# A convolution and gate taken through PSUM by halves, and a product left in its bank until its sums

## The chip, the cores and the metric

The kernel runs on one core of one Trainium2 chip. The metric is the device time of one execution in microseconds (us); what is quoted for a kernel is the median of its runs. The engines have short names in the profile: PE is TensorE's matrix products (PEld its weight loads), DVE is VectorE, ACT is ScalarE, POOL is GpSimd, SP is SyncE, which here only issues DMAs. PSUM has eight banks of 128 partitions by 512 float32 numbers; products land there, VectorE and ScalarE read and write it, POOL does not use it in this kernel.

## The reference, cut to what matters

One layer of a decoder trunk on 2048 tokens of 1024 features. The change touches its feed-forward part alone:

```python
h = h + conv_ffn(rms_norm(h, ln2_g), w_up, conv_w, conv_b, w_down)
return rms_norm(h, lnf_g)

def conv_ffn(h, w_up, conv_w, conv_b, w_down):
    up = h @ w_up                              # 1024 -> 2 * 2816
    up = causal_depthwise_conv(up, conv_w)     # three taps along the tokens
    up = up + conv_b
    gate, val = up[..., :2816], up[..., 2816:]
    return (silu(gate) * val) @ w_down         # 2816 -> 1024
```

Ahead of it stand the input projection, attention over a window, and a state space model; they are not changed.

## The kernel before, in words

The program is one long list of instructions for each engine. A scheduler that knows the dependences puts them in order ahead of time by modelled durations; on the chip each engine runs its own list strictly in order and waits at semaphores. Buffers come from pools: a tile of a name gets the next free buffer of that name, and its first writer waits for the last user of the buffer's previous tile.

The kernel runs in passes. Passes A to D make the input projection, state space and attention, with h, the tokens after attention, kept in device memory. Pass E is the feed-forward up to the product of gate and value, pass F the product down and the last norm.

In E and F every matrix product is cut in two along each dimension and computed with seven products of blocks instead of eight (Winograd's form of Strassen's method). The seven are M1 to M7, in the order M1, M5, M6, M7, M2, M3, M4 (`n` = 0 to 6 in `pair`). One operand is fixed for a pass (r0 to r6, built by `fixed` from blocks loaded into the staging buffers sg0 and sg1, both `sg` in the profile), the other comes by steps (`moving`, sums in the tile `sums`). Each operand is float32 and is split into a high and a low half (`split`: a cast on ScalarE, a subtraction, here on POOL for the steps' operands); a product of blocks is therefore 12 matrix instructions of 512 columns where four blocks are summed over (9 where three are). The split halves of the steps' operands go around five buffer sets: sq, ath, atl, xt, ln.

Pass E goes over two halves of 1024 tokens, and in each over 22 steps of 128 gate and 128 value features, taken in pairs: 11 pairs a half. Pass F goes over three groups of features (blocks of 4, 4 and 3), each over 8 steps of 256 tokens, again in pairs. So there are 22 pairs in E and 12 in F, with the fixed operands replaced four times on the way. `pass_of` runs a pass; while its last pair's products run, the next pass's fixed operands are built one after the other behind the last product that uses the old one (`nxt` in `pair`).

`pair` puts each product into a PSUM bank (eight banks taken in rotation, L1057) and takes it out again: M1 and M5 are copied by ScalarE (L1075), the others are added by VectorE to a running sum in SBUF (L1078). After M7, C12 gets M5 by an addition on POOL (L1080) and C22 by one on VectorE (L1081), both between SBUF tiles. The places c are halves of the tiles u: `yl` (gate) and `sm_` (value) of 1024 tokens and two tokens before.

`up_end` runs the convolution for a step: for gate and value a first tap with bias on ScalarE into a tile `xh` (L1148), two more taps on VectorE (L1149, L1150, listed as L118), Silu of the gate on ScalarE (L1151), the product of both on VectorE (L1152, listed as L115), and one store to `act_d`. Lines 115, 118 and 133 are helpers (`tt_`, `stt_`, `split`), so many instructions of the profile carry these lines, and are told apart by their tiles. In F, `more` adds the tokens h (tile `xh`) to the sums, two quarters on VectorE and two on POOL.

Of the kernel before, what the change touches and what calls it, by code (L numbers as in the profile page):

```python
# [9 lines left out]
F32 = mybir.dt.float32  # L10
# [6 lines left out]
P = 128  # L17
L = 2048
D = 1024
# [22 lines left out]
def constants():  # L42
    """Tables that depend on shapes alone: identity, band masks, shifts, rotary angles."""
# [25 lines left out]
def trunk(ctx, tc, a, out):  # L69
# [50 lines left out]
    def rstd_of(ss, n):  # L120
        """1/sqrt(ss/n + eps): a power refined by one Newton step."""
# [9 lines left out]
    def split(hi, lo, x, eng=None):  # L131
        """x as the sum of two numbers that the tensor engine takes whole."""
        S.copy(out=hi, in_=x)  # L133
        tt_(lo, x, f(hi), ALU.subtract, eng)

    # ================ pass A: first norm, input projection; the state space's matrices ================
# [49 lines left out]
    def norm_in(g):  # L186
        """Normed tokens, turned, as exact halves."""
# [42 lines left out]
    def proj_qkv(b, hi, lo):  # L230
# [14 lines left out]
        # rotary on the first 16 of each head's features  # L245
# [8 lines left out]
        # queries and keys as exact halves: a head's halves side by side, the keys' each twice  # L254
# [7 lines left out]
        # values and their differences to the block before  # L262
# [14 lines left out]
    def pass_a(g):  # L277
        """A pair of blocks: its state space's input, and queries, keys and values of the pair before."""
        hnT[g] = norm_in(g)
        if 0 < g < NB // 2 - 1:  # L280
            both_qkv(g - 1)
        proj_u(g, *hnT[g])
# [10 lines left out]
    # heads of a group: the even ones, then the odd ones  # L293
# [76 lines left out]
    # sine and cosine: to the nearest multiple of pi/2, then by polynomials  # L370
# [26 lines left out]
    # by quadrant: swapped where odd, then signs  # L397
# [16 lines left out]
    # powers 0..8 of the discrete eigenvalues  # L414
# [22 lines left out]
    # input matrices, (lam_bar - 1) / lam times b  # L437
# [19 lines left out]
    # by half of the partitions (real parts, imaginary parts)  # L457
# [12 lines left out]
    # phase of a chunk, doubled seven times  # L470
# [6 lines left out]
    # two groups to a table: the first's phases on the lower partitions, the second's on the upper  # L477
# [26 lines left out]
    def tables(j):  # L504
        """Cosines and sines, cosines and negated sines of a chunk's phase by its number, for two groups."""
# [17 lines left out]
    def matrices(j):  # L523
        """A chunk's matrices, for GB groups: input to state, state to output; for twice as many,
        input to output."""
# [54 lines left out]
    # ================ pass B: the state space; attention and its part of the output ================  # L580
# [26 lines left out]
    def ssm(j):  # L607
        """The state space for GB groups."""
# [66 lines left out]
    def padded(t, x, kv, r):  # L675
        """A head's values on one half of the partitions to be, zeros on the other."""
# [3 lines left out]
    def attention(b):  # L680
# [5 lines left out]
        for kv in range(NKV):  # L686
            # key slots: this block's where it is no later than the query, else the previous one's
# [37 lines left out]
            else:  # L725
                # all weights on the previous block's values, this block's weights on the differences
# [18 lines left out]
    def attention_in(b):  # L745
        (q, k), idr = qkvs.pop(b), idrs[0]
        # turned: a head's halves of queries over each other, against its group's keys' halves, twice each
# [36 lines left out]
    # values between zeros: a head's product lands on the lower or the upper half of the partitions  # L784
# [11 lines left out]
    def out_half(th, tl, wh, wl, done, nms=("pi", "pi")):  # L796
        """Rows of one half of the output projection for a block of tokens."""
# [16 lines left out]
    def sumsq(t):  # L814
        """Squares of a block's features, for their sums by token."""
# [28 lines left out]
    def load_gate():  # L844
        """Weights of the state space's gate and of its half of the output projection."""
# [89 lines left out]
    # ================ pass D: the state space's gate, its part of the output, second norm ================  # L935
# [345 lines left out]
```

## Time and profile before

| | us |
|---|---|
| three runs | 2229.15 to 2231.34, median 2230.11 |
| span of the profiled execution, first to last instruction | 2223.6 |
| the profiled execution's own time | not given apart from its span |
| PE busy | 2034.0 (91%) |
| DVE busy | 1810.5 (81%) |
| POOL busy | 1473.9 (66%) |
| ACT busy | 1002.3 (45%) |
| mean granted clock of TensorE | 0.961 of full speed |

Busy time is the sum of the durations of an engine's instructions, including any time in which an instruction was held up while it ran. The page's slices of the span show PE at 9 tenths in most of the second half, with dips near 1220 to 1300, 1680 to 1770 and 1890 to 1940 us. Pass E begins at about 781 us, between the last parts of D, its second half at about 1253, and F at about 1717.

### The profile page before, as it was taken

The page shows a single profiled execution, that of the slowest core. Times are in us where ns is not written, and L with a number is a line of the kernel's source. Part 1 is how long each engine was busy: PE and PEld are TensorE (multiplying, and loading weights), DVE is VectorE, ACT ScalarE, POOL GpSimd, SP SyncE. Part 2 cuts the span into 40 slices and gives each one's busy share as a digit, 9 for nine tenths or more (in the row PEclk, how much of TensorE's full clock was granted, in tenths as well). Part 3 has the DMA queues.
Part 4 walks back from the last instruction along what each step waited for, and adds up shares of the span by engine and source line. Part 5 has one row for each costly group of instructions (what it writes and reads, how often), then busy time and mean ns, then how long its engine had stood idle before and what let it go on. Part 6 is the DMA issues. An engine that isn't in the chain of part 4 may idle for free.

```text
span 2223.6 us, 29721 instructions
## 1 busy us (share of the span) xinstructions
PE 2034.0 (91%) x10057; PEld 1695.7 (76%) x10057; DVE 1810.5 (81%) x2491; ACT 1002.3 (45%) x2007; POOL 1473.9 (66%) x1247
## 2 busy tenths in 40 slices
PE   7899977999899889999999789999997899899896
PEld 6789967888788778887777568878776687688664
DVE  6987368999876768878788987878889968767898
ACT  5575346555556544434434343444434423233333
POOL 2556325766631556676776976776778879888985
PEclk9999988999999999999999899999999899899998
DMA  7476386777556752232332323231323455464543
GB/s 213 155 259 251 125 276 221 223 230 217 160 173 202 216 169 71 82 90 67 92 108 69 121 76 96 67 103 59 122 86 122 149 184 171 170 218 148 183 156 139
DMA packets 304621, 335.49 MB, mean 151 GB/s; under 512 B 92070, under 2 KB 237910, under 8 KB 302934
## 3 DMA queue, kind: packets, MB, share of 16 engines
q1 hardware_dynamic: 304470, 333.60, 46.7%
q8 instruction: 80, 1.31, 0.2%
q14 instruction: 71, 0.58, 0.1%
HBM read 214.14 MB, written 119.41 MB: 150 GB/s over the span
## 4 chain that ended last, share of the span: by engine, by line
PE 29%; DVE 16%; POOL 9%; issue 6%; DMA 4%; ACT 2%; DVEq 0%; ACTq 0%; SPq 0%; POOLq 0%
PE pz L1071 7%; PE ps L1071 7%; DVE xh L118 6%; PE po L1071 4%; PE pi L1071 4%; PE px L1071 3%; PE pp L1071 3%; DVE sums L115 3%; DMA yh<-in_w_up_dram 2%; POOL yl L115 1%; POOL atl L115 1%; POOL ath L115 1%; ACT xh L1148 1%; POOL sq L115 1%; POOL ln L115 1%
## 5 line engine op out<-in xcount | busy, mean ns | idle before, releaser
L1148 ACT ACTIVATE xh<-yl,cb,cw 128x1024 f32<-128x1024 f32 x44 | 54.8, 1245 | 244.6 <-DVE yl L115 144.7
L118 DVE SCALAR_TENSOR_TENSOR xh<-yl,cw,xh 128x1024 f32<-128x1024 f32 x88 | 145.5, 1653 | 13.3 <-ACT xh L1148 12.2
L115 POOL TENSOR_TENSOR rs<-rs,mhalf 128x1 f32<-128x1 f32 x80 | 51.8, 654 | 157.3 <-DVE rs L112 151.1
L115 POOL TENSOR_TENSOR atl<-sums,atl 128x512 fp32r<-128x512 f32 (+1 forms) x40 | 68.2, 1705 | 30.1 <-ACT atl L133 30.0
L115 POOL TENSOR_TENSOR ln<-sums,ln 128x512 fp32r<-128x512 f32 (+1 forms) x43 | 70.0, 1627 | 24.4 <-ACT ln L133 20.0
L115 POOL TENSOR_TENSOR sq<-sums,sq 128x512 fp32r<-128x512 f32 (+1 forms) x42 | 73.2, 1743 | 19.4 <-ACT sq L133 18.7
L115 POOL TENSOR_TENSOR xt<-sums,xt 128x512 fp32r<-128x512 f32 (+1 forms) x39 | 58.8, 1508 | 33.1 <-ACT xt L133 33.1
L1151 ACT ACTIVATE xh<-xh 128x1024 f32<-128x1024 f32 x44 | 46.7, 1062 | 72.2 <-DVE xh L118 72.2
L115 DVE TENSOR_TENSOR sums<-yt 128x512 f32<-128x512 f32 (+1 forms) x48 | 64.8, 1352 | 16.5 <-POOL xt L115 7.1
L115 DVE TENSOR_TENSOR xh<-xh 128x1024 f32<-128x1024 f32 x44 | 76.2, 1732 | 1.8
L218 PE MATMUL pz<-hnT_lo,wu_h 128*128 128x256 f32 x256 | 73.8, 291 | 2.6 <-DVE hnT_lo L115 2.6
L218 PE MATMUL pz<-hnT_hi,wu_h 128*128 128x256 f32 x256 | 72.1, 291 | 2.1 <-ACT hnT_hi L133 2.0
L218 PE MATMUL pz<-hnT_hi,wu_l 128*128 128x256 f32 x256 | 72.7, 287 | 0.0
L115 POOL TENSOR_TENSOR sq<-sq 128x256 f32<-128x256 f32 (+1 forms) x64 | 42.5, 678 | 41.6 <-ACT sq L817 41.1
L115 POOL TENSOR_TENSOR vv<-vv 128x255 f32<-128x255 f32 x32 | 26.3, 822 | 64.6 <-DVE vv L115 59.5
L115 POOL TENSOR_TENSOR ath<-sums,ath 128x512 fp32r<-128x512 f32 (+1 forms) x40 | 64.6, 1615 | 5.0 <-ACT ath L133 5.0
L115 DVE TENSOR_TENSOR sums<-yt,yh 128x512 f32<-128x512 f32 x44 | 48.1, 1093 | 23.0 <-DMA yh<-in_w_up_dram 21.9
L115 DVE TENSOR_TENSOR sg<-sg,sg 128x2048 f32<-128x2048 f32 (+1 forms) x20 | 54.9, 2743 | 13.3 <-DMA sg<-in_w_down_dram 8.6
L709 ACT ACTIVATE s<-s,m 128x128 f32<-128x128 f32 x120 | 46.9, 392 | 40.8 <-DVE m L118 40.8
L804 PE MATMUL pi<-w_oh,ath 128*128 128x512 f32 x128 | 55.1, 430 | 7.4 <-DVE rs L112 5.3
L115 POOL TENSOR_TENSOR mh<-th,cc 128x512 fp32r<-128x512 f32 x30 | 42.0, 1400 | 24.9 <-ACT th L133 24.8
L115 POOL TENSOR_TENSOR atl<-yh,atl 128x512 fp32r<-128x512 f32 (+1 forms) x29 | 47.6, 1642 | 15.3 <-ACT atl L133 9.7
(1963 smaller groups left out, 8294.5 us busy)
## 6 DMA issues: line engine op xcount, KB each, us to landing
xh<-h_d SPq DMA_DIRECT2D x48, 512.0 KB, 4.3
yt<-in_w_up_dram SPq DMA_DIRECT2D x44, 512.0 KB, 4.6
yh<-in_w_up_dram SPq DMA_DIRECT2D x44, 512.0 KB, 3.7
act_d<-xh SPq DMA_DIRECT2D x44, 512.0 KB, 3.1
h_d<-yl SPq DMA_DIRECT2D x32, 512.0 KB, 3.7
qk_d<-qx SPq DMA_DIRECT2D x16, 768.0 KB, 3.2
sg<-h_d SPq DMA_DIRECT2D x12, 1024.0 KB, 6.8
sg<-in_w_down_dram SPq DMA_DIRECT2D x12, 1024.0 KB, 5.8
```

Of the source, the lines that this page charges most:

```text
L115: (eng or V).tensor_tensor(out=o, in0=x, in1=y, op=op)
L118: V.scalar_tensor_tensor(out=o, in0=x, scalar=s, in1=y, op0=o0, op1=o1)
L218: E.matmul(out=pu, lhsT=l["u"][:, k, cs], rhs=r[:, k, :], start=n == 0, stop=n == 3 * KT - 1)
L709: S.activation(out=s[:, h], in_=s[:, h], func=AF.Exp, bias=m[:, h:h + 1], accum_out=den[:, h:h + 1])
L804: E.matmul(out=po, lhsT=l[:, k, :], rhs=r[k][:, cs], start=n == 0, stop=n == 11)
L1071: E.matmul(out=b, lhsT=l[:, k], rhs=r[:, k], start=m == 0, stop=m == 3 * kh - 1)
L1148: S.activation(out=v, in_=u[s_][:, 2:], func=AF.Identity, scale=w2, bias=cb[:, fc_:fc_ + 1])
L1151: S.activation(out=ds[0], in_=ds[0], func=AF.Silu)
```

## The change

In `pair`, a product's bank is chosen by its number: M5 (`n == 1`) and M3 (`n == 5`) take `pi` and `po` in turn, all others `ps` and `pz` in turn, of which there are two buffers each. `pp` and `px`, one buffer each, are left to the convolution. M5 is no longer copied out; its bank is kept until M7 is there, and both sums with M5 are then made by VectorE from the bank. In the last step of F both sums were on VectorE before, too.

In `up_end` the convolution runs by halves of 512 tokens. The first tap goes to the bank `pp` (gate) or `px` (value), the other two taps run on VectorE from bank to bank, Silu reads `pp` and writes SBUF, the product reads `px` and writes SBUF.

```diff
-    banks, turn = ("pz", "ps", "pi", "po", "pz", "ps", "pp", "px"), [0]
-
-    def pair(ops, res, cs, nxt=None, more=None, eng=None):
+    turn = [0, 0]
+
+    def mm_bank(n):
+
+        k = int(n == 1)
+        turn[k] += 1
+        return bank((("ps", "pz"), ("pi", "po"))[k or n == 5][turn[k] % 2], [P, HF])
+
+    def pair(ops, res, cs, nxt=None, more=None):
+
+        m5 = {}
...
-                b = bank(banks[turn[0] % 8], [P, HF])
-                turn[0] += 1
+                b = mm_bank(n)
...
-                if n < 2:
-                    S.copy(out=c[3 * n], in_=b)
+                if n == 0:
+                    S.copy(out=c[0], in_=b)
+                elif n == 1:
+                    m5[s_] = b
                 else:
                     o, i = ((1, 0), (2, 1), (0, 0), (1, 1), (2, 2))[n - 2]
                     tt_(c[o], b, c[i], ALU.add)
                 if n == 3:
-                    tt_(c[1], c[1], c[3], ALU.add, eng or Q)
-                    tt_(c[3], c[3], c[2], ALU.add)
+                    tt_(c[3], m5[s_], c[2], ALU.add)
+                    tt_(c[1], m5.pop(s_), c[1], ALU.add)
...
-        ds = [oa.tile([P, HT], F32, name="xh") for _ in range(2)]
-        for s_ in range(2):
-            fc_ = s_ * NF + fx
-            w0, w1, w2 = (cw[:, t * 2 * NF + fc_:t * 2 * NF + fc_ + 1] for t in range(3))
-            v = ds[s_]
-            S.activation(out=v, in_=u[s_][:, 2:], func=AF.Identity, scale=w2, bias=cb[:, fc_:fc_ + 1])
-            stt_(v, u[s_][:, 1:HT + 1], w1, v, ALU.mult, ALU.add)
-            stt_(v, u[s_][:, 0:HT], w0, v, ALU.mult, ALU.add)
-        S.activation(out=ds[0], in_=ds[0], func=AF.Silu)
-        tt_(ds[1], ds[0], ds[1], ALU.mult)
+        act = oa.tile([P, HT], F32, name="xh")
+        for j in range(2):
+            o = j * HF
+            for s_ in range(2):
+                fc_ = s_ * NF + fx
+                w0, w1, w2 = (cw[:, t * 2 * NF + fc_:t * 2 * NF + fc_ + 1] for t in range(3))
+                v = bank(("pp", "px")[s_], [P, HF])
+                S.activation(out=v, in_=u[s_][:, o + 2:o + 2 + HF], func=AF.Identity, scale=w2, bias=cb[:, fc_:fc_ + 1])
+                stt_(v, u[s_][:, o + 1:o + 1 + HF], w1, v, ALU.mult, ALU.add)
+                stt_(v, u[s_][:, o:o + HF], w0, v, ALU.mult, ALU.add)
+                x = act[:, o:o + HF]
+                if s_ == 0:
+                    S.activation(out=x, in_=v, func=AF.Silu)
+                else:
+                    tt_(x, v, x, ALU.mult)
```

The rest of the diff takes out comments and the argument `eng`. What the scheduler makes of it is seen in the engines' lists. On VectorE, in the fifth pair of the first half of E, these rows stand where the convolution of the pair before ends and the sums of this one begin (a name is a tile with its number; `<-` names what is read); before:

```order
L118 SCALAR_TENSOR_TENSOR xh_10824<-yl_10537,cw_69,xh_10824 128x1024 x2
L118 SCALAR_TENSOR_TENSOR xh_10825<-sm__10538,cw_69,xh_10825 128x1024 x2
L115 TENSOR_TENSOR xh_10825<-xh_10824,xh_10825 128x1024
L115 TENSOR_TENSOR yl_10835<-pz_10932,yl_10835 128x512
L115 TENSOR_TENSOR yl_10839<-ps_10951,yl_10839 128x512
L115 TENSOR_TENSOR sm__10836<-pp_10969,yl_10835 128x512
L115 TENSOR_TENSOR sm__10840<-px_10988,yl_10839 128x512
L115 TENSOR_TENSOR sm__10836<-sm__10836 128x512
```

In the changed kernel, at the same place:

```order
L118 SCALAR_TENSOR_TENSOR px_10899<-sm__10598,cw_69,px_10899 128x512 x2
L115 TENSOR_TENSOR xh_10893<-px_10899,xh_10893 128x512
L118 SCALAR_TENSOR_TENSOR px_10909<-sm__10598,cw_69,px_10909 128x512 x2
L115 TENSOR_TENSOR yl_10915<-pz_11010,yl_10915 128x512
L115 TENSOR_TENSOR xh_10893<-px_10909,xh_10893 128x512
L115 TENSOR_TENSOR yl_10919<-ps_11029,yl_10919 128x512
L115 TENSOR_TENSOR sm__10916<-pz_11047,yl_10915 128x512
L115 TENSOR_TENSOR sm__10916<-po_10974,sm__10916 128x512
L115 TENSOR_TENSOR yl_10915<-po_10974,yl_10915 128x512
```

The convolution's steps are half as wide and read and write px; the first sums of the new pair stand among them; the two last rows are the sums with M5, read from its bank po.

On POOL, in the same pair, the low halves of the steps' operands, before:

```order
L115 TENSOR_TENSOR ath_11041<-sums_10847,ath_11040 128x512
L115 TENSOR_TENSOR atl_11060<-sums_10870,atl_11059 128x512
L115 TENSOR_TENSOR yl_10835<-yl_10835,sm__10836 128x512
L115 TENSOR_TENSOR xt_11077<-yh_10845,xt_11077 128x512
L115 TENSOR_TENSOR yl_10839<-yl_10839,sm__10840 128x512
L1142 COPY cc_66<-sm__10836 128x2
```

And in the changed kernel:

```order
L115 TENSOR_TENSOR ath_11119<-sums_10927,ath_11118 128x512
L115 TENSOR_TENSOR atl_11138<-sums_10950,atl_11137 128x512
L1150 COPY cc_66<-sm__10916 128x2
L115 TENSOR_TENSOR xt_11155<-yh_10925,xt_11155 128x512
L1150 COPY cc_66<-sm__10920 128x2
L115 TENSOR_TENSOR ln_11172<-yh_10948,ln_11172 128x512
```

The two sums into yl are gone from POOL; the rest keeps its order.

On VectorE at the change from the first to the second half of E, where r0 and r2 of the new fixed operands get their low halves (r0l, r2l) and sg0 its subtraction, before:

```order
L118 SCALAR_TENSOR_TENSOR xh_12642<-yl_12355,cw_69,xh_12642 128x1024
L115 TENSOR_TENSOR r0l_12708<-sg0_12321,r0h_12707 128x1024
L118 SCALAR_TENSOR_TENSOR xh_12643<-sm__12356,cw_69,xh_12643 128x1024 x2
L115 TENSOR_TENSOR yl_12653<-pz_12763,yl_12653 128x512
L115 TENSOR_TENSOR xh_12643<-xh_12642,xh_12643 128x1024
L115 TENSOR_TENSOR yl_12657<-ps_12782,yl_12657 128x512
L115 TENSOR_TENSOR sg0_12796<-sg0_12796,sg1_12323 128x2048
L115 TENSOR_TENSOR sm__12654<-pi_12809,yl_12653 128x512
L115 TENSOR_TENSOR r2l_12800<-sg0_12796,r2h_12799 128x1024
```

And in the changed kernel:

```order
L115 TENSOR_TENSOR r0l_12908<-sg0_12479,r0h_12907 128x1024 x2
L118 SCALAR_TENSOR_TENSOR px_12837<-sm__12536,cw_69,px_12837 128x512 x2
L115 TENSOR_TENSOR xh_12831<-px_12837,xh_12831 128x512
L115 TENSOR_TENSOR yl_12853<-pz_12961,yl_12853 128x512
L118 SCALAR_TENSOR_TENSOR px_12847<-sm__12536,cw_69,px_12847 128x512
L115 TENSOR_TENSOR sg0_12994<-sg0_12994,sg1_12481 128x2048
L118 SCALAR_TENSOR_TENSOR px_12847<-sm__12536,cw_69,px_12847 128x512
L115 TENSOR_TENSOR yl_12857<-ps_12980,yl_12857 128x512
L115 TENSOR_TENSOR xh_12831<-px_12847,xh_12831 128x512
L115 TENSOR_TENSOR r2l_12998<-sg0_12994,r2h_12997 128x1024
```

Both halves of r0l now stand ahead of the last value steps, and the sums from PSUM (yl from pz and ps) are nearer to each other in the list.

## Rows read from the trace of the kernel before

**Rows 1.** The page, part 1: busy time of each engine and its share.

```profile
PE 2034.0 (91%) x10057; PEld 1695.7 (76%) x10057; DVE 1810.5 (81%) x2491; ACT 1002.3 (45%) x2007; POOL 1473.9 (66%) x1247
```

**Rows 2.** Busy us (x instructions) by stretch, then granted clock, DMA share, GB/s.

```profile
880.82:1201.71 320.89, 313.67 (x1345) 252.42 (x1344) 263.04 (x241) 131.95 (x193) 224.04 (x193) 0.99 0.28 86
1201.71:1310.84 109.13, 87.77 (x338) 68.65 (x336) 101.72 (x71) 46.61 (x63) 91.00 (x55) 0.89 0.31 97
1310.84:1663.53 352.69, 349.75 (x1513) 283.23 (x1512) 295.81 (x268) 146.50 (x213) 252.34 (x179) 1.00 0.28 87
1663.53:1771.95 108.42, 87.86 (x337) 68.19 (x336) 102.29 (x72) 46.59 (x63) 94.39 (x47) 0.91 0.35 117
1771.95:1897.69 125.74, 119.70 (x511) 96.97 (x510) 96.72 (x82) 38.50 (x62) 109.08 (x66) 0.97 0.53 182
1897.69:2067.96 170.27, 159.60 (x671) 128.34 (x670) 127.11 (x107) 54.84 (x88) 145.40 (x88) 0.96 0.54 184
2067.96:2204.00 136.04, 119.54 (x478) 92.28 (x477) 122.48 (x182) 54.24 (x129) 116.11 (x94) 0.95 0.48 163
2204.00:2223.60 19.60, 5.92 (x24) 4.38 (x23) 15.16 (x32) 2.71 (x9) 2.32 (x4) 0.76 0.29 107
```

**Rows 3.** Timeline, TensorE: start us, us, engine, line, operation, output<-inputs, partitions x columns.

```profile
972.37 0.39 PE L1071 MATMUL pz<-r2h,sq 128*128 128x512 f32 x1
...
1427.15 0.39 PE L1071 MATMUL pi<-r0h,sq 128*128 128x512 f32 x1
...
1465.73 0.39 PE L1071 MATMUL pz<-r0h,ln 128*128 128x512 f32 x1
```

**Rows 4.** Line 118 on VectorE: count, ns shortest/median/longest, first and last start, form.

```profile
L118 DVE SCALAR_TENSOR_TENSOR xh<-yl,cw,xh x88: 1272/1287/3386, 840.7 to 1744.2; 128x1024 f32<-128x1024 f32 x88
...
L118 DVE SCALAR_TENSOR_TENSOR yl<-po,rs,yl x16: 716/739/751, 635.8 to 797.8; 128x512 f32<-128x512 f32 x16
```

**Rows 5.** Timeline, VectorE, 982 to 996 us (in brackets: idle before, and until whom).

```profile
982.33 0.68 DVE L115 TENSOR_TENSOR yl<-pz,yl 128x512 f32<-128x512 f32 x1
...
983.53 0.68 DVE L115 TENSOR_TENSOR sm__10836<-pp,yl 128x512 f32<-128x512 f32 x1
984.13 0.68 DVE L115 TENSOR_TENSOR sm__10840<-px,yl 128x512 f32<-128x512 f32 x1
987.36 1.77 DVE L115 TENSOR_TENSOR sm__10836<-sm__10836 128x512 f32<-128x512 f32 x1 [2.56 <-POOL yl L115]
...
995.82 0.69 DVE L115 TENSOR_TENSOR sums<-yh,yt 128x512 f32<-128x512 f32 x1
```

**Rows 6.** Timeline, POOL, 983 to 990 us.

```profile
983.52 1.31 POOL L115 TENSOR_TENSOR ath<-sums,ath 128x512 fp32r<-128x512 f32 x1
984.76 1.32 POOL L115 TENSOR_TENSOR atl<-sums,atl 128x512 fp32r<-128x512 f32 x1
...
988.51 1.78 POOL L115 TENSOR_TENSOR yl<-yl,sm__10840 128x512 f32<-128x512 f32 x1
```

**Rows 7.** Staging tile sg on VectorE and on POOL: counts and ns as in rows 4.

```profile
L115 DVE TENSOR_TENSOR sg<-sg,sg x20: 2251/2604/4548, 738.1 to 2065.0; 128x2048 f32<-128x2048 f32 x16, 128x1536 f32<-128x1536 f32 x4
...
L115 DVE TENSOR_TENSOR r5l<-sg,r5h x2: 1218/1222/1226, 815.4 to 816.5; 128x1024 fp32r<-128x1024 f32 x2
...
L115 POOL TENSOR_TENSOR r4l<-sg,r4h x2: 2409/2905/3401, 800.1 to 802.5; 128x1024 fp32r<-128x1024 f32 x2
```

**Rows 8.** Bank po on VectorE: counts and ns as in rows 4.

```profile
L562 DVE CAST dm<-po x8: 1101/1142/1166, 114.9 to 228.6; 128x512 fp32r<-128x512 f32 x8
```

**Rows 9.** Waits from 1201.71 to 1310.84: us in total, times, longest.

```profile
ACT r3h L133 <- DVE sg L115: 7.7, 1, 7.7
...
PE px L1071 <- POOL ln L115: 4.9, 1, 4.9
```

**Rows 10.** Line 1148 on ScalarE: count and ns as in rows 4.

```profile
L1148 ACT ACTIVATE xh<-yl,cb,cw x44: 1239/1245/1252, 839.4 to 1740.3; 128x1024 f32<-128x1024 f32 x44
```

**Rows 11.** The page, part 6: DMAs, count, KB each, median us to landing.

```profile
sg<-h_d SPq DMA_DIRECT2D x12, 1024.0 KB, 6.8
```

More of the change, by code (lines that the diff above doesn't have):

```diff
@@ L1142, in up_end @@
                 Q.tensor_copy(out=carry[:, fx, i], in_=u[i][:, HT:HT + 2])
-        ds = [oa.tile([P, HT], F32, name="xh") for _ in range(2)]
-        for s_ in range(2):
-            fc_ = s_ * NF + fx
-            w0, w1, w2 = (cw[:, t * 2 * NF + fc_:t * 2 * NF + fc_ + 1] for t in range(3))
-            v = ds[s_]
-            S.activation(out=v, in_=u[s_][:, 2:], func=AF.Identity, scale=w2, bias=cb[:, fc_:fc_ + 1])
-            stt_(v, u[s_][:, 1:HT + 1], w1, v, ALU.mult, ALU.add)
-            stt_(v, u[s_][:, 0:HT], w0, v, ALU.mult, ALU.add)
-        S.activation(out=ds[0], in_=ds[0], func=AF.Silu)
-        tt_(ds[1], ds[0], ds[1], ALU.mult)
+        act = oa.tile([P, HT], F32, name="xh")
[13 more added lines that the diff above has]
+                    tt_(x, v, x, ALU.mult)
         Y.dma_start(out=act_d[hb * 4:hb * 4 + 4, :, fx, :].rearrange("q p t -> p q t"),
-                    in_=ds[1].rearrange("p (q t) -> p q t", t=2 * P))
+                    in_=act.rearrange("p (q t) -> p q t", t=2 * P))
     KG = [(0, 4), (8, 4), (16, 3)]
@@ L1245, in steps @@
                 hs, cs, more = zip(*ps_)
-                return [dn_step(q + i, f0, kh) for i in range(w)], (cs, hs, more, V if last else None)
+                return [dn_step(q + i, f0, kh) for i in range(w)], (cs, hs, more)
             def end(hs):
```

## The prediction, before the changed kernel ran

> **What bounds the kernel now.** I read the page first. TensorE is busy 91% of the span [rows 1], so the question is where the other 9% lies. The windows by stage answer that [rows 2]. A pair of steps at its best repeats every 38.58 us (first product at 1427.15, the next pair's at 1465.73 [rows 3]). That is 14 products of 2.756 us with no gap, at full granted clock, and serves as the floor. Against it: eight pairs of the first half take 320.89 (floor 308.6, loss 12.3); nine of the second 352.69 (347.2, loss 5.5); the change from first to second half of the tokens, two pairs, 109.13 (77.2, loss 32.0); the change from pass E to F, two pairs, 108.42 (77.2, loss 31.2); the next seven pairs of F 125.74 + 170.27 = 296.0 (270.1, loss 25.9); the last group, products a quarter shorter, 136.04 (115.7, loss 20.3). The granted clock is 0.89 and 0.91 in the two changes, near 1.00 in the steady stretches. Together 127 us are lost between 880.82 and 2204; the 19.60 behind that is the last norm.
>
> Who is late there? At the first change TensorE waits longest for POOL's low halves [rows 9]. POOL and VectorE are both nearly full (91.00 and 101.72 of 109.13), but full of what? The same VectorE form, 1024 columns with both tensors in SBUF, takes from 1.27 to 3.39 us, while forms with one tensor in PSUM keep 0.72 to 0.75 [rows 4]. In the timeline 512-column adds from PSUM run at 0.60 from start to start (983.53, 984.13 [rows 5]) although POOL works through 983.52 to 984.8 [rows 6]; an SBUF add takes 1.77 when POOL is at work (987.36), 0.69 when it isn't. POOL's own 512-column form is 1.25 from start to start undisturbed, and 1.78 beside that SBUF add. I read this as turns: a POOL operation and a VectorE operation on two SBUF tensors don't advance together; one on PSUM is free of it.
>
> So I add up turns alone, at undisturbed prices: POOL 512 columns 1.25; VectorE 512 columns 0.60, 1024 columns 1.28 - 0.08 = 1.20 (rows overlap by 0.08, as 0.68 against 0.60 shows). A pair of pass E: POOL 14 splits and 2 sums (L1080) = 16 x 1.25 = 20.0; VectorE 8 convolution steps and 2 gate products of 1024 = 12.0, 2 sums (L1081) and 8 operand sums = 10 x 0.60 = 6.0. Sum 38.0 beside a floor of 38.58: both are full. The fixed operands of a new pass add on POOL 8 x 2.4 = 19.2, on VectorE 3 x 2.25 + 6 x 1.22 = 14.1 [rows 7], 33.3 in all. Two pairs and that: 109.3, measured 109.13. Seven pairs of F (POOL 20 x 1.25, VectorE 14 x 0.60 = 33.4 each) with 33.3 for one operand set and 25 for the shorter one after it: 292 against 296.0. This sum fits three stages within 2%, so the turns, not either engine's work, set the losses.
>
> **The change part by part.** *Convolution in PSUM.* Per pair, 8 steps and 2 products of 1024 columns on two SBUF tensors become 16 and 4 of 512 with the second tensor in PSUM. Turns lost: 12.0 us per pair. VectorE's own time: the nearest row is a scalar-times-tensor operation from PSUM, 0.74, and a plain one, 0.68 [rows 4, 5], so 16 x 0.74 + 4 x 0.68 = 14.6 against 12.0 undisturbed and far more disturbed. No row has VectorE writing PSUM; below, 0.60 each (12.0); above, the slowest 512-column row that touches PSUM, 1.14 [rows 8], gives 22.8. I take 14.6, the nearest form. VectorE per pair is then 14.6 + 10 drains and 4 sums from PSUM x 0.60 + 8 operand sums x 0.60 = 27.8 of 38.58 (36 at the upper bound: still under).
>
> ScalarE: the first tap was 1.245 for 1024, now two of 512 into PSUM; half is 0.62 [rows 10]. Per pair 8 taps, 4 Silu, 14 casts and 2 copies, 28 forms of 512 columns, at 0.62 make 17 us of 38.58, so they hide; at twice the price for the 8 that write PSUM, 22. The Trainium skill (ScalarE: Activation LUTs, Step-by-step: what each stage is for) says an ACTIVATE into PSUM is faster than into SBUF, useful only if TensorE doesn't need most of PSUM. No run here shows the first half yet; the sum would move by less than 1 us. The second half is a rival below.
>
> Two waits are added: a tap into pp waits for the Silu that empties it, one into px for the product. Behind the tap stand ScalarE's casts for the next operands, some 0.6 us each with four operands of lead; I cost them at nothing while VectorE keeps up. The store of a step stays one transfer, after its second product.
>
> *The fifth product stays.* Per pair 2 copies leave ScalarE (1.2 us, hidden), 2 sums leave POOL (2.5 us of turns), 2 VectorE SBUF sums become PSUM sums (1.2 us of turns), and 2 new VectorE sums of 0.60 come. In F the same.
>
> *Banks.* A step's products come in the order M1, M5, M6, M7, M2, M3, M4, each for both steps of a pair. Eight banks in rotation become four (ps, pz) for all but M5 and M3, two (pi, po) for these, and pp, px for the convolution. At the tightest place, from M6 to M2, a bank of the four is wanted again three products after its own ended, 8.25 us; M5's bank has as long from the end of M7 to M3. Before, there were seven products between, 19.3 us.
>
> *New sums.* E pair: 14 x 1.25 + 8 x 0.60 = 22.3 us of turns, floor 38.58. A change of pass: 44.6 + 33.3 = 77.9, floor 77.2. Seven pairs of F: 7 x (18 x 1.25 + 12 x 0.60 = 29.7) + 58.3 = 266, floor 270.1. So nowhere do turns exceed the floor by more than 1 us, and what is late next is the chain of a fixed operand through its two staging buffers: after the second operand's products end (11 us into the last pair) cast 2, low half 4.8, load 6.8 [rows 11], subtract 2.3, cast and low half 6.8, load 6.8, cast and low half 4.5, load 6.8, cast and low half 6.8 = 59 us, wanted at 38.6 + 27.6 = 66. Three of its pieces stand in POOL's queue behind up to three splits of 1.25 each: some 11 us, 4 too late, and a stall costs clock. I leave 10 us of loss at each change.
>
> **Sum.** Steady pairs of E: of 17.7 lost, three quarters come back, -13. Changes: 32.0 to 10, -22; 31.2 to 10, -21. F: turns and TensorE are both full there (266 beside 270), so of 25.9 half stays, -13; the last group 20.3 to 13, -7. Before 880 and the last norm 0: pass D is untouched, and the last steps already had this sum on VectorE. Total -76. The span goes from 2223.6 to 2148. The runs' median of 2230.1 is 6.5 above that span (the profiled execution's own time is not given apart), so I forecast 2154.
>
> **Rivals.** *The chain sets the changes.* If POOL's queue makes the fixed operands later than I think, each change keeps 22 and F its losses: -13 - 10 - 9 - 6 = -38, 2192. For: ScalarE waited 7.7 us for a subtraction into r3h in the first change [rows 9]; against: that subtraction stood behind convolution steps of over 3 us which now lose their turns.
>
> *Everything goes.* If the turns alone made all the losses, some 120 of 127 go: 2110. Against: loads and clock dips at the changes have causes of their own.
>
> *Four banks are too few (slower).* The drain of M6 shows the danger: the first step's ended about 972.8 [rows 3] and was drained from 982.33 [rows 5], 9.5 us later; the new rotation allows 8.25. VectorE is in order, and a convolution step that waits for ScalarE (one pp, one px, four rounds each per pair) holds the drains queued behind it. If each of eight rounds stands idle some 0.9 us, VectorE's 27.8 become 35, drains come 4 us beyond the allowance, and TensorE stops as long in each of 22 pairs: +88, against 63 gained outside the steady pairs: 2255. It decides from about 2.9 us a pair. By the Trainium skill (PSUM — Partial Sum Buffer, Summary: rules for kernel authors) banks are to be emptied promptly since PSUM is tight; by that rule this is the outcome. Against, in the order of instructions: the drains of M6 now stand among halves of some 0.7 us rather than behind two pairs of 1024-column steps, and before them steps on pp and px alternate, so that one bank's wait is filled by the other's work.
>
> *No such turns.* If the long VectorE rows come from something else, PSUM operands gain nothing and the time stays within 5 us of 2230.
>
> **How the numbers follow.** Forecast 0.62, chain 0.14, everything 0.10, four banks 0.11, no turns 0.03. The range 2112 to 2205 holds the first three but the best end of the third and leaves out the last two. What a measurement can tell is 0.2%, 4.5 us: faster 0.86, same 0.03, slower 0.11.
>
> **What would show it.** Right: steps on pp and px at 0.7 to 0.8 whatever POOL does; POOL's 512-column splits near 1.3; pairs of E at 38.6 throughout; the two changes at 82 to 92 us; seven pairs of F near 283. Wrong: TensorE waiting for VectorE's drains in steady pairs (four banks); changes still above 97 with POOL or loads named (chain); POOL's splits still at 1.7 (no turns). A price of PSUM writes above 1.14 would break the sum too.

## The result, and the profile after

| | median, us | runs | ratio to before, 95% interval |
|---|---|---|---|
| before | 2229.63 | 4, 2225.27 to 2231.34 | |
| changed | 2154.95 | 4, 2153.82 to 2157.45 | 0.9663 [0.9644, 0.9681] |

The forecast was 2154, in a range of 2112 to 2205. The span of the profiled execution fell from 2223.6 to 2152.9 us. The page, part 1, of the changed kernel (columns as in [rows 1]):

```profile
PE 2003.9 (93%) x10057; PEld 1681.7 (78%) x10057; DVE 1681.9 (78%) x2778; ACT 1013.6 (47%) x2071; POOL 1238.0 (58%) x1180
```

POOL is busy 236 us less and VectorE 129 us less, though VectorE has 287 instructions more. Of POOL's 236 us the sums that left it, 44 in E and 23 in F, explain about 84 at 1.25 each; the rest is shorter instructions of the same form. The changed kernel's lines of VectorE's convolution steps and of ScalarE's first tap, the gate's (columns as in [rows 4]):

```profile
L118 DVE SCALAR_TENSOR_TENSOR pp<-yl,cw,pp x176: 737/750/757, 838.7 to 1693.4; 128x512 f32<-128x512 f32 x176
...
L1158 ACT ACTIVATE pp<-yl,cb,cw x88: 765/783/797, 837.9 to 1691.8; 128x512 f32<-128x512 f32 x88
```

The spread is what to read: 737 to 757 ns over all of pass E, where [rows 4] had 1272 to 3386. POOL's split of sums into sq in the first half of E, in the kernel before:

```profile
L115 POOL TENSOR_TENSOR sq<-sums,sq x8: 1296/1884/2282, 896.0 to 1167.6; 128x512 fp32r<-128x512 f32 x8
```

and in the changed kernel:

```profile
L115 POOL TENSOR_TENSOR sq<-sums,sq x8: 1288/1292/1297, 892.4 to 1154.9; 128x512 fp32r<-128x512 f32 x8
```

So the change in VectorE's operands made POOL's untouched instructions a third shorter here. The windows by stage, which answer to [rows 2] (eight pairs of E, change, nine pairs, change, seven pairs of F, last group, tail):

```profile
883.52:1192.21 308.69, 308.69 (x1345) 252.36 (x1344) 235.50 (x337) 140.46 (x224) 159.57 (x177) 1.00 0.29 89
1192.21:1277.33 85.12, 80.13 (x338) 64.38 (x336) 78.20 (x92) 46.25 (x69) 68.99 (x47) 0.96 0.40 124
1277.33:1624.61 347.28, 347.28 (x1514) 283.94 (x1513) 265.85 (x381) 159.00 (x254) 174.24 (x164) 1.00 0.29 88
1624.61:1712.77 88.16, 80.53 (x338) 63.71 (x337) 82.26 (x89) 43.84 (x65) 71.25 (x42) 0.98 0.45 153
1712.77:1994.34 281.57, 273.61 (x1178) 221.46 (x1176) 201.58 (x200) 85.10 (x133) 227.36 (x137) 0.99 0.53 187
1994.34:2141.34 147.00, 125.25 (x505) 95.69 (x503) 126.28 (x202) 53.00 (x126) 103.06 (x89) 0.97 0.47 163
2141.34:2152.90 11.56, 0.00 (x0) 0.00 (x0) 6.93 (x19) 2.06 (x6) 1.06 (x2) 0.70 0.24 91
```

In the first and third row TensorE is busy as long as the stretch lasts: every pair takes 38.6 us, the floor. The table sets the profiled kernels side by side; a stage is cut where a pair's last product ends and the next one's first begins in TensorE's timeline, to some 0.2 us. Before's last product ends at 2209.92, not at the 2204 where [rows 2] cut. Two profiles, of the additions on POOL and of those from PSUM, fell in executions with a granted clock of 0.75 instead of 0.96 and have no row, and these two executions and one of before at 2302.12 us stay out of the medians too.

| us | 8 pairs from | 8 pairs E | change | 9 pairs E | change | 7 pairs F | last group | tail |
|---|---|---|---|---|---|---|---|---|
| before | 880.8 | 320.9 | 109.1 | 352.7 | 108.4 | 296.0 | 142.0 | 13.7 |
| changed | 883.5 | 308.7 | 85.1 | 347.3 | 88.2 | 281.6 | 147.0 | 11.6 |
| convolution alone | 885.0 | 308.8 | 90.6 | 346.9 | 88.6 | 295.9 | 144.3 | 13.7 |
| fifth product alone | 884.5 | 311.0 | 100.7 | 347.4 | 99.5 | 282.4 | 147.1 | 11.6 |
| halves in SBUF | 888.6 | 309.3 | 103.3 | 347.3 | 104.8 | 281.2 | 146.7 | 11.6 |
| before, six banks | 882.7 | 320.6 | 109.1 | 354.3 | 105.9 | 297.2 | 142.7 | 13.8 |
| before, additions on VectorE | 883.0 | 331.8 | 110.2 | 377.1 | 119.4 | 295.9 | 144.5 | 13.7 |
| changed, once more | 882.0 | 308.7 | 85.5 | 347.3 | 87.8 | 282.1 | 147.1 | 11.6 |
| changed, additions on POOL | 881.9 | 308.7 | 88.5 | 347.3 | 91.9 | 281.4 | 146.7 | 11.6 |
| changed, six banks in F | 882.8 | 308.7 | 85.1 | 347.3 | 94.0 | 282.2 | 149.2 | 9.5 |
| changed, low halves on VectorE | 886.8 | 308.7 | 88.8 | 347.3 | 91.4 | 278.1 | 147.0 | 11.6 |
| changed, edits in F | 884.9 | 308.7 | 85.5 | 347.3 | 88.0 | 278.1 | 144.3 | 15.3 |

(A change is two pairs, and what the pair behind it takes beyond 38.6, where that is over 0.5. Two pairs of E lie ahead of the first column's time. Additions and edits are those of the experiments below.)

What TensorE waits for in the changed kernel, from 1190 to 1278 and, below the dots, from 1994.34 to 2141.34 (us in total, times, longest):

```profile
PE ps L1077 <- POOL ln L115: 4.5, 1, 4.5
PE po L1077 <- POOL ath L115: 0.5, 1, 0.5
...
PE ps L1077 <- DVE yl L115: 4.8, 1, 4.8
PE ps L1077 <- ACT yl L1081: 4.7, 2, 3.4
PE pi L1077 <- DVE yl L115: 4.1, 1, 4.1
```

For the steady pairs of E the same view is empty. At the first change TensorE still waits for POOL; at the second its longest wait is 3.0 us, for VectorE; in the last group it waits for VectorE and ScalarE, the engines that empty its banks.

### The profile page after: what moved, and what is told of

Read it like the earlier page. It is cut to its first block, busy times and chain, and to the rows that moved or that the text cites. A ratio compares the mean times of both kernels' runs of the same rounds, so it can differ in the third digit from the quotient of the medians.

```text
span 2152.9 us, 29873 instructions
## 1 busy us (share of the span) xinstructions
PE 2003.9 (93%) x10057; PEld 1681.7 (78%) x10057; DVE 1681.9 (78%) x2778; ACT 1013.6 (47%) x2071; POOL 1238.0 (58%) x1180
## 3 DMA queue, kind: packets, MB, share of 16 engines
q8 instruction: 80, 1.31, 0.2%
## 4 chain that ended last, share of the span: by engine, by line
PE 48%; DVE 8%; POOL 4%; issue 2%; DMA 2%; ACT 1%; DVEq 0%; ACTq 0%; POOLq 0%
PE ps L1077 17%; PE pz L1077 17%; PE pi L1077 7%; PE po L1077 6%; DMA sg<-in_w_down_dram 1%; DVE sums L115 1%; DVE yl L115 1%; DVE sg L115 1%; DVE yl L118 1%; DVE rs L118 1%; POOL xt L115 1%; POOL ln L115 1%; DVE rs L115 1%; PE pi L804 0%; PE po L804 0%
## 5 line engine op out<-in xcount | busy, mean ns | idle before, releaser
L118 DVE SCALAR_TENSOR_TENSOR pp<-yl,cw,pp 128x512 f32<-128x512 f32 x176 | 131.9, 750 | 38.5 <-ACT pp L1158 37.9
L1163 ACT ACTIVATE xh<-pp 128x512 f32<-128x512 f32 x88 | 52.7, 598 | 93.9 <-DVE pp L118 93.0
L1158 ACT ACTIVATE pp<-yl,cb,cw 128x512 f32<-128x512 f32 x88 | 69.0, 784 | 53.9 <-DVE yl L115 52.9
L115 DVE TENSOR_TENSOR yl<-pz,yl 128x512 f32<-128x512 f32 x66 | 45.3, 686 | 49.6 <-PE pz L1077 47.2
L115 POOL TENSOR_TENSOR atl<-sums,atl 128x512 fp32r<-128x512 f32 (+1 forms) x40 | 56.2, 1404 | 33.2 <-ACT atl L133 33.1
L115 POOL TENSOR_TENSOR ln<-sums,ln 128x512 fp32r<-128x512 f32 (+1 forms) x43 | 55.8, 1299 | 31.5 <-ACT ln L133 30.9
L115 POOL TENSOR_TENSOR sq<-sums,sq 128x512 fp32r<-128x512 f32 (+1 forms) x42 | 54.7, 1303 | 27.6 <-ACT sq L133 26.0
L115 POOL TENSOR_TENSOR sq<-sq 128x256 f32<-128x256 f32 (+1 forms) x64 | 42.7, 680 | 42.0 <-ACT sq L817 39.6
L115 DVE TENSOR_TENSOR xh<-px,xh 128x512 f32<-128x512 f32 x88 | 60.5, 687 | 1.9
L115 POOL TENSOR_TENSOR xt<-yh,xt 128x512 fp32r<-128x512 f32 (+1 forms) x28 | 41.5, 1480 | 28.5 <-ACT xt L133 28.4
L115 DVE TENSOR_TENSOR yl<-ps,yl 128x512 f32<-128x512 f32 x70 | 47.9, 685 | 11.3 <-PE ps L1077 10.0
```

What stands on the lines that cost most here:

```text
L115: (eng or V).tensor_tensor(out=o, in0=x, in1=y, op=op)
L118: V.scalar_tensor_tensor(out=o, in0=x, scalar=s, in1=y, op0=o0, op1=o1)
L1158: S.activation(out=v, in_=u[s_][:, o + 2:o + 2 + HF], func=AF.Identity, scale=w2, bias=cb[:, fc_:fc_ + 1])
L1163: S.activation(out=x, in_=v, func=AF.Silu)
```

## Experiments

Each was timed beside the kernel before on its chip.

### The convolution by halves in PSUM, alone

The kernel before, with the changed `up_end`, and its products in rotation over six banks since pp and px are taken:

```diff
-    banks, turn = ("pz", "ps", "pi", "po", "pz", "ps", "pp", "px"), [0]
+    banks, turn = ("pz", "ps", "pi", "po", "pz", "ps"), [0]
```

> The kernel before with the convolution by halves in pp and px alone; M5 is copied out and its two sums stay on POOL and VectorE between SBUF tiles; products go round the other six banks. Turns theory: a pair of E needs 16 x 1.25 + 10 x 0.60 = 26 us of turns, below the floor of 38.58, so steady pairs are at the floor (-17 us in all) and the two changes of E need 2 x 26 + 33.3 = 85 instead of 109, some -17 each; F keeps its 33.4 us a pair and gains nothing. About 2178 us. Rival 'POOL's two sums': they alone held the kernel back, so this one is at 2225 to 2230. Rival 'halves': as fast as the changed kernel in E, the same 2175 to 2185.

Measured 2175.33 (2169.55 to 2180.40), ratio 0.975 [0.9728, 0.9772]. The steady pairs stand at the floor and both changes are almost as short as in the changed kernel; F stays as it was.

### The fifth product in its bank, alone

The changed kernel with the convolution of before (1024 columns, SBUF).

> The changed kernel with the old convolution (1024 columns, SBUF tiles): M5 held in its bank alone. Turns theory: a pair of E needs 14 x 1.25 + 12.0 + 8 x 0.60 = 34.3 us of turns, just under the floor: steady pairs near 38.6, changes 2 x 34.3 + 33.3 = 102 instead of 109; F gains as in the changed kernel (some -14). About 2190 us. Rival 'POOL's two sums': nearly the whole gain, 2155 to 2165. Rival 'halves': only F's share and the copy's, 2210 to 2220.

Measured 2186.22 (2183.72 to 2189.94), ratio 0.9801 [0.9785, 0.9817]. F gains its 14 us here, and the steady pairs of E too come within 3 us of the floor, but the changes stay at 100. Both parts alone gain 55.1 and 44.2, together 75: the steady pairs can be gained once only.

### Halves, but in SBUF

```diff
-        act = oa.tile([P, HT], F32, name="xh")
+        ds = [oa.tile([P, HT], F32, name="xh") for _ in range(2)]
+        act = ds[1]
...
-                v = bank(("pp", "px")[s_], [P, HF])
+                v = ds[s_][:, o:o + HF]
...
-                x = act[:, o:o + HF]
+                x = ds[0][:, o:o + HF]
...
-                    tt_(x, v, x, ALU.mult)
+                    tt_(v, x, v, ALU.mult)
```

> The changed kernel with its convolution by halves of 512, but into SBUF tiles instead of pp and px. Turns theory: the turns are those of M5 alone, 34.3 us a pair: about 2190 us, within 8 us of that kernel; the taps on VectorE range from 0.74 to over 1.5 us. Rival 'halves' (smaller pieces let the sums from PSUM through earlier, wherever the taps lie): 2155 to 2165, as the changed kernel.

Measured 2193.20 (2190.86 to 2194.78), ratio 0.983 [0.9815, 0.9845]. The convolution's steps, ScalarE's tap and POOL's split in this kernel:

```profile
L118 DVE SCALAR_TENSOR_TENSOR xh<-yl,cw,xh x176: 734/751/2830, 842.9 to 1725.4; 128x512 f32<-128x512 f32 x176
...
L1159 ACT ACTIVATE xh<-yl,cb,cw x88: 797/816/827, 840.4 to 1722.2; 128x512 f32<-128x512 f32 x88
...
L115 POOL TENSOR_TENSOR sq<-sums,sq x8: 1284/1668/1894, 903.6 to 1162.1; 128x512 fp32r<-128x512 f32 x8
```

Same engines, same widths, same number of instructions as the changed kernel; only the place of the tensor `v` differs, and with it the buffers: two tiles `xh` a step instead of one tile and two banks. What the wait for these buffers adds is not separated. The undisturbed step costs the same (median 751 against 750 ns), but the longest is 2830 against 757, POOL's split is at 1668 against 1292, and the median is 38 us longer. Of the 39.7 by which the spans differ, 34.8 lie in the two changes; 5.1 lie ahead of the eight pairs, 4.7 of them already at E's first product (788.3 against 783.5), where the start scatters from kernel to kernel. So some 35 us are the place's. The cut into halves gives nothing by itself: the kernel with 1024 columns in SBUF took 2186.22.

### Six banks, nothing else

The rotation of the first experiment in the kernel before.

> The kernel before with six banks in rotation instead of eight (pp and px unused in E and F). Turns theory: turns are the same, a bank is still free for five products, 13.8 us, more than the 10 us that the latest drain took: 2225 to 2235 us. Rival 'banks': the kernel before already lived on its eight banks, so it loses 10 us or more.

Measured 2228.65 (2223.74 to 2234.61), ratio 0.9992 [0.998, 1.0004]: two banks fewer cost nothing there.

### Additions on POOL, on VectorE, and on VectorE from PSUM

Four unused additions in each pair of E, in three forms, one of the three lines in each kernel (`scr` is a tile of zeros):

```diff
+                    if more is None and n in (4, 5):
+                        tt_(scr[:, 0], c[o], scr[:, 1], ALU.add, Q)   # on POOL
+                        tt_(scr[:, 0], c[o], scr[:, 1], ALU.add)      # on VectorE
+                        tt_(scr[:, 0], b, scr[:, 1], ALU.add)         # on VectorE, from the bank
```

> The kernel before, with four more 512-column additions on POOL in each pair of pass E, all on SBUF tiles (88 in all; their result is not used). Turns theory: a steady pair's turns go from 38.0 to 38.0 + 4 x 1.25 = 43.0 us, 4.4 above TensorE's floor of 38.58, and all of that shows: about +95 us over 22 pairs, 2325 (2300 to 2345). Rival (POOL has a third of its time idle, and what is late is something else): within 10 us of before, 2230 to 2240.

> As the run with POOL's additions, but the same four additions per pair stand on VectorE, from SBUF to SBUF. Turns theory: 4 x 0.60 = 2.4 us of turns more per pair, 40.4 beside a floor of 38.58: about +50 us, 2280 (2260 to 2290). Rival (VectorE has a fifth of its time idle, so they fit): within 10 us, 2230 to 2240.

> As the run with VectorE's additions, but one of the two tensors of each is read from the product's PSUM bank instead of from SBUF; as many instructions of the same width on the same engine. Turns theory: no turn is used, VectorE has the room: within 12 us of before, 2230 to 2242. Rival (it is VectorE's own time or the length of its queue that is short, not turns): as much as with SBUF tiles, 2260 to 2290.

| before, with 88 additions | median, us | ratio, 95% interval | over before (2227.90) |
|---|---|---|---|
| on POOL | 2285.76 | 1.0265 [1.0233, 1.0298] | +57.9 |
| on VectorE, SBUF | 2278.81 | 1.0232 [1.0212, 1.0252] | +50.9 |
| on VectorE, one from PSUM | 2255.61 | 1.0118 [1.0089, 1.0146] | +27.7 |

The turns theory as I had priced it held for one of the three. POOL, with a third of its time idle, has no room for 110 us more, so that rival falls; but 58 came, not 95. And VectorE additions that use no turn cost 28, not at most 12. By the same count and width, the place of one tensor is worth 23 us, the instruction's place on VectorE 28. That the latter comes from VectorE's in-order list (busy 83% of the span in the run with SBUF tiles) is argued; that the additions keep their banks longer is a rival that was not run, though two banks fewer cost nothing above. The additions in SBUF, in the kernel with 2278.81:

```profile
L115 DVE TENSOR_TENSOR scr<-yl,scr x88: 676/685/2892, 840.2 to 1766.8; 128x512 f32<-128x512 f32 x88
```

Half of them run undisturbed at 685 ns or less; the others are held, and all 88 together take some 46 us more than at 676 ns each.

### The same additions on POOL in the changed kernel

> The changed kernel with the same 88 additions on POOL as in the run with POOL's additions. Turns theory: 22.3 + 5.0 = 27.3 us of turns per pair stay under the floor of 38.58, so they cost next to nothing in steady pairs and at most some us at the changes: 2155 to 2170. Rival (POOL's low halves are on the path by themselves): some 4 us in each pair as before the change, 2230 to 2255.

Measured 2161.40 (2159.77 to 2162.99), ratio 0.9704 [0.9686, 0.9723], some 6 us over the changed kernel. All steady pairs stay at 38.6; the two changes take 7.1 us more, and the eight pairs begin 1.6 sooner. The same load on POOL costs 58 us in the kernel before and some 7 in the changed one.

### More banks in F

```diff
+        if wide and n not in (1, 5):
+            turn[2] += 1
+            return bank(("ps", "pz", "pp", "ps", "pz", "px")[turn[2] % 6], [P, HF])
...
-                b = mm_bank(n)
+                b = mm_bank(n, more is not None)
```

> The changed kernel, but in pass F, where the convolution no longer uses pp and px, the products other than M5 and M3 rotate over six banks (ps, pz, pp, ps, pz, px) instead of four. If the last group's 5 us more than before come from the four banks (TensorE waits for ScalarE's copies, which wait for stores, and for VectorE's sums), TensorE's waits for VectorE and ScalarE on banks (some 13 us there) go, the last group falls from 147 to some 138 us and the whole to 2142 to 2148. Rival (operands that come late set the last group, the banks only show it): within 4 us of the changed kernel, 2151 to 2159.

Measured 2162.92 (2160.57 to 2166.35), ratio 0.971 [0.969, 0.973]. Nearer to the rival, but above its range too, and 8 us above the changed kernel beside it (2155.11): the last group takes 149 us and its tail 9.5, together as long as before the edit, with TensorE's waits there now on the banks of M5 and M3:

```profile
PE pi L1080 <- DVE yl L115: 7.2, 2, 4.1
PE po L1080 <- DVE yl L115: 5.2, 3, 2.5
PE pz L1080 <- POOL xt L115: 1.7, 1, 1.7
```

The wait was moved, not removed: VectorE's sums are late, and TensorE stands at whichever bank comes next. The change from E to F is 5.8 us longer. Waits of TensorE from 1640 to 1760 in the same kernel:

```profile
PE po L1080 <- ACT sq L133: 4.2, 1, 4.2
PE pp L1080 <- ACT atl L133: 2.8, 1, 2.8
PE pp L1080 <- ACT xh L1166: 2.7, 1, 2.7
```

The last row is a product of F that wants pp while the last convolution has it, until its Silu (L1166) ends. The other two waits end with ScalarE's casts of operands. The first of them cost 1.5 us in the changed kernel, the second lies in the pair behind; why these casts are later here is not shown.

### Low halves of the fixed operands on VectorE

```diff
-    def fixed(load, kh, les="VQVQVQQ"):
+    def fixed(load, kh, les="VVVVVVV"):
```

> The changed kernel, but the low halves of the fixed operands at the four changes are all subtracted on VectorE (1.2 us for 1024 columns) instead of four of seven on POOL (2.4). If POOL's queue, in which the steps' low halves stand behind those of the fixed operands, sets what is left at the changes (TensorE waited 4.5 and 4.2 us for ln), the two changes fall from 85 and 88 us towards 80, F by some us, and the whole to 2140 to 2150. Rival (VectorE, busy 78 and 82 us of these changes, is the fuller of the two): drains come later and it is slower, 2157 to 2175.

Measured 2160.13 (2158.67 to 2161.43), ratio 0.9694 [0.9676, 0.9713]. F's seven pairs gain 3.5 us, but the two changes lose 3.7 and 3.2, and not above all to drains by VectorE. The wait for POOL's ln is gone from both. TensorE's longest waits in the first change of this kernel:

```profile
PE pz L1077 <- ACT yl L1081: 7.0, 1, 7.0
PE ps L1077 <- ACT yl L1081: 1.7, 1, 1.7
```

and three rows of ScalarE's timeline there (in brackets: idle before, and until whom):

```profile
1244.44 2.00 ACT L133 CAST r6h<-sg 128x1024 fp32r<-128x1024 f32 x2 [0.61 <-DVE sg L115]
...
1254.11 1.99 ACT L133 CAST r5h<-sg 128x1024 fp32r<-128x1024 f32 x2 [6.63 <-DMA sg<-h_d]
...
1257.72 0.57 ACT L1081 COPY yl<-pz 128x512 f32<-128x512 f32 x1
```

The copy that empties M1's bank now stands on ScalarE behind the cast of r5, which waits 6.63 us for its load. In the changed kernel's timeline that copy came between the casts:

```profile
1241.16 1.99 ACT L133 CAST r6h<-sg 128x1024 fp32r<-128x1024 f32 x2
1243.05 0.58 ACT L1081 COPY yl<-pz 128x512 f32<-128x512 f32 x1
...
1252.11 1.98 ACT L133 CAST r5h<-sg 128x1024 fp32r<-128x1024 f32 x2
```

The second change has the same wait of 7.0 us, there with 4.81 us for a load in front of the cast. So the first theory's wait went, as it said, and a longer one that neither theory has came in its place: an order that the scheduler chose anew put a copy behind a load.

### The changed kernel once more

> The changed kernel once more, beside the two runs with six banks in F and with the low halves on VectorE: 2153 to 2158, ratio to before 0.966.

Measured 2155.11 (2152.53 to 2156.27), ratio 0.9672 [0.9653, 0.9691]. Its stages repeat the changed kernel's within 2 us each.

### Two edits in F together

In the changed kernel, the last group takes M5 out by a copy and rotates over eight banks as before, and the second and third group's low halves go to VectorE:

```diff
+                elif n == 1 and kh == 3:
+                    S.copy(out=c[3], in_=b)
...
+                if n == 3 and kh == 3:
+                    tt_(c[1], c[1], c[3], ALU.add, eng or Q)
+                    tt_(c[3], c[3], c[2], ALU.add)
...
-[fixed(dn_load(*g), g[1]) for g in KG]
+[fixed(dn_load(*g), g[1], "VVVVVVV" if g[0] else "VQVQVQQ") for g in KG]
```

> The changed kernel with two edits in F: low halves of the fixed operands of the second and third group all on VectorE (where that took 4 us off seven pairs of F, while it cost 3.5 at each change to a pass before), and in the last group the fifth product copied out and eight banks in rotation as before the change. If the loss of 5 us in the last group comes from keeping M5, the group goes from 147 back to 142 to 144 us and the whole, with the 4 us of the low halves, to 2146 to 2150. Rival (the last group is as long either way, because its operands and its norm are late, and the two kernels with the old F that were run, at 144.2 and 144.4 us with a tail of 13.7, show no more than 1 us): only the low halves' 4 us, 2150 to 2153.

Measured 2153.05 (2147.67 to 2155.00), ratio 0.9654 [0.9637, 0.967]. Its interval overlaps the changed kernel's, so it is no version shown to be faster. The rows of its F (seven pairs, last group, tail) say why:

```profile
1714.40:1992.50 278.10, 272.66 (x1176) 221.25 (x1174) 212.05 (x210) 86.84 (x135) 199.81 (x127) 0.99 0.54 193
1992.50:2136.80 144.30, 126.36 (x504) 94.56 (x504) 129.47 (x196) 54.68 (x130) 104.06 (x89) 0.98 0.46 155
2136.80:2152.10 15.30, 0.00 (x0) 0.00 (x0) 10.88 (x25) 2.67 (x8) 1.10 (x2) 0.65 0.28 103
```

The low halves' gain, 3.5 us, is there. The last group is shorter by 2.7 and the tail longer by 3.7: the rival holds, at the edge of its range. (A third kernel with the old F that had run, six banks, stood at 142.7 with a tail of 13.8.)

## Why the prediction was right, step by step

*That turns set the losses: right.* Turns against no turns was decided by the halves in SBUF (some 35 us for the place of one tensor) and by POOL's additions (58 us in the one kernel, 7 in the other). The three signs named beforehand are there: steps at 737 to 757 ns, POOL's splits at 1.29 us, steady pairs at 38.6. By the Trainium skill (SBUF — State Buffer, SBUF: two separate sides) VectorE and GpSimd share a port pair that whichever starts first holds for its whole instruction, VectorE where it has two inputs in SBUF (against a GpSimd instruction that reads SBUF) or runs in a two-port mode; the splits at 1668 and 1292 ns above agree.

*That a pair of E is full of turns at 38.0 us: right.* Two rows of POOL's timeline before, between those of [rows 6]:

```profile
986.01 1.32 POOL L115 TENSOR_TENSOR yl<-yl,sm__10836 128x512 f32<-128x512 f32 x1
987.26 1.32 POOL L115 TENSOR_TENSOR xt<-yh,xt 128x512 fp32r<-128x512 f32 x1
```

VectorE's addition at 987.36 [rows 5] starts 0.10 us after POOL's split of 987.26 and ends 0.55 after it; POOL's next sum, at 988.51 [rows 6], ends 1.16 after that addition. Each ran when the other had ended. So whole durations from start to start are the price; the 1.77 - 0.69 = 1.08 and 1.78 - 1.31 = 0.47 us by which these two are longer than undisturbed are what was left of the other's when they started. The sums on record can be set beside a count over the eight pairs: the time in which POOL was in an instruction, or VectorE in one without a tensor in PSUM, merged from the timelines. If the two advanced together, this time would fall short of the sum of their undisturbed prices.

| us by pair of E | turns, forecast | counted | the pair took |
|---|---|---|---|
| before | 38.0 | 37.8 | 40.1 |
| before, additions on VectorE | 40.4 | 39.6 | 41.5 |
| fifth product alone | 34.3 | 34.3 | 38.9 |
| halves in SBUF | 34.3 | 35.1 | 38.7 |
| changed, additions on POOL | 27.3 | 27.7 | 38.6 |
| convolution alone | 26 | 27.3 | 38.6 |
| changed | 22.3 | 24.0 | 38.6 |

At the first change the count is 52.9 of 54.6 us by pair before, 49.1 of 51.7 with the halves in SBUF, 37.8 of 42.6 in the changed kernel.

*From turns to time: too simple.* Steady pairs of before take 39.6 us on average though their turns come to 38.0 and TensorE needs 38.58: two lists in order, each late by the other, lose some time before the turns fill the pair. That is argued, no run takes a list away. My forecasts for the additions counted what exceeds 38.58. Counted from the 39.6 where the pairs stood, with 17 steady pairs and four at the changes (an estimate made afterwards), VectorE's four additions of 0.60 give 23 us and POOL's, at the 1.114 measured below, 66. For POOL 58 came. For VectorE 51 came: 23 is what the place of one tensor was worth, and the other 28, which the additions from PSUM cost as well, stand outside the turns, their cause open. That 2280 was met there was luck.

*Steady pairs: 13 forecast, 17.6 came* (320.9 + 352.7 to 308.7 + 347.3). All of the loss went, since either part alone nearly ends it.

*The two changes: 22 and 21 forecast, 24.0 and 20.3 came.* What I said would be late next was a chain of casts, low halves and loads. My sum of turns there had three subtractions between staging buffers for a set of fixed operands; [rows 7] has 20 for five sets, four each. That makes 35.6 us a set instead of 33.3, so a change needs 80.2 us of turns beside TensorE's 77.2, 3 us over and not 1 (75.5 were counted at the first). The wait left at the first change is for POOL's ln, 4.5 us; the chain of work that ended last runs there through r6's low halves to ln on POOL (start us, us, what):

```profile
1242.28 0.93 POOL r6l L115
...
1245.52 3.33 POOL r6l L115
1248.85 1.68 POOL ln L115
1250.57 4.63 PE ps L1077 x10
```

So the steps' operands stand behind the fixed ones in POOL's queue, as predicted. To move the low halves off POOL took this wait away, but not the time: a wait for a copy took its place.

*F's seven pairs: 13 forecast, 14.4 came,* all from the fifth product: 295.9 with the convolution alone, 282.4 with the fifth product alone.

*The last group, 7 us forecast, is the term that was mis-sized: with its tail it grew from 155.7 to 158.6.* First the cut was wrong: TensorE's last product ended 6 us behind my 2204, so the loss of 20.3 was not what it seemed. Then fewer turns did not shorten it, and nothing else that was tried shortened group and tail together. Four kernels have before's code in this stage, two of them with six banks instead of eight: 155.7 (before), 156.5 (six banks), 158.0 (convolution alone) and 158.2 (additions on VectorE). The rest took 158.3 to 159.6. So of the 2.9 us up to 2.5 are what the same code shows from one kernel to another. What sets this stage stays open; the last products' sums and the norm of the last tokens are in it, and VectorE is busy 126 of its 147 us.

*Outside the stages.* The eight pairs begin 2.7 us later, where I had put 0; among the kernels run this start lies between 880.8 and 888.6, and E's first product between 781.1 and 788.3, though pass D is the same in all, which no run explains. And the 6.5 us by which the median stood above the span were too much: later executions lie some 2 above theirs (2154.16 with a span of 2152.0). The span fell by 70.7 instead of 76; the smaller offset gives 4.5 back, so that the forecast was met within 1 us in part by luck.

*ScalarE's tap: 0.62 forecast, 0.783 measured.* It hides, as said. Half of the 1.245 us of [rows 10] was no fair price for a halved instruction: the same 512 columns into SBUF took 0.816 (halves in SBUF), 0.033 more than into PSUM. So the sentence of the Trainium skill (ScalarE: Activation LUTs, Step-by-step: what each stage is for), that an ACTIVATE into PSUM is faster, is borne out, by 4%. VectorE's step, 0.74 forecast, was 0.750.

*Four banks too few: wrong in E, with a trace of it in F.* No steady pair waits at all. In the last group, and in the kernel with a copy behind a load, TensorE does stop at full banks, for up to 7 us at a time. The rule to empty banks promptly (the Trainium skill, PSUM — Partial Sum Buffer, Summary: rules for kernel authors) did not decide the time.

## What to carry to other kernels

Where VectorE and POOL are both busy, look for the same form at very different lengths; if forms with a PSUM operand keep theirs, put one operand of VectorE's two-tensor instructions in PSUM, before moving work between the two engines. Price such a conflict by whole durations from start to start, and check the sum by the merged time in which either engine is at work. What a load adds is counted from where the stage stands, not from its floor, and an instruction that uses no turn is not free either (28 us for 88 here). A stage is cut at the end of its last product, and a tail counts with the stage before it.

## What the runs showed of the hardware that was not expected

A 512-column scalar-times-tensor step on VectorE with input and output in PSUM takes 0.750 us, as long as from SBUF to SBUF undisturbed (0.751). A 512-column ScalarE tap with scale and bias by partition takes 0.783 us into PSUM and 0.816 into SBUF, against 1.245 for 1024 columns into SBUF. The 88 added float32 additions of 512 columns on POOL take 1.114 us in the changed kernel. A split of that width, which writes float32 rounded for TensorE, takes 1.29, but so does a plain float32 sum (1.32 at 986.01 above): the output's type does not explain the difference, and what does is not shown. The added ones:

```profile
L115 POOL TENSOR_TENSOR scr<-yl,scr x88: 1086/1114/2066, 837.4 to 1677.8; 128x512 f32<-128x512 f32 x88
```
